# Output projection, plain blocks and first product pair of a hybrid decoder block: the passage between them in another order

## The chip, the core and the metric

The kernel runs on one core of a Trainium2 chip. Five engines work on their own queues: TensorE (PE) multiplies, VectorE (DVE) and ScalarE (ACT) do elementwise work, GpSimd (POOL) and SyncE (SP) issue transfers here. Each queue is worked off in order, and instructions wait for each other by semaphores. The metric is the time of one execution in microseconds (us); lower is better.

## What is computed

A decoder block over 1024 positions of width 1024, float32: a state-space branch and a gated convolution branch, merged by gates and projected, then a squared-ReLU MLP. Cut to what matters here (the mixer's inner part left out):

```python
def rmsnorm(x, g):
    var = jnp.mean(x * x, axis=-1, keepdims=True)
    return x * lax.rsqrt(var + NORM_EPS) * g
...
    merged = jax.nn.sigmoid(g_ssm) * y_a + jax.nn.sigmoid(g_conv) * y_b
    return jnp.einsum('bsd,de->bse', merged, w_out)
...
def squared_relu_mlp(xn, w_ff1, w_ff2):              # w_ff1: 1024 x 4096
    h = jax.nn.relu(jnp.einsum('bsd,df->bsf', xn, w_ff1))
    return jnp.einsum('bsf,fd->bsd', h * h, w_ff2)
...
    h = h + mixer_block(rmsnorm(h, norm_mix_g), ...)
    h = h + squared_relu_mlp(rmsnorm(h, norm_mlp_g), w_ff1, w_ff2)
    return rmsnorm(h, norm_final_g)
```

## The kernel before

Everything is kept transposed: 128 channels on the partitions, positions along the row, in two halves of 512 (`HS[0]`, `HS[1]`). A float32 product is made of three TensorE passes: each operand is split into a high part (ScalarE copies it to a rounded type) and a low part (VectorE subtracts the high part), and high x high, low x high and high x low are added up in one PSUM bank (a 128x512 float32 buffer; there are eight). So a split is always a ScalarE instruction followed by a VectorE one.

The order of each engine's queue is the order in which the code is written; nothing reorders it. The stretch that the change touches goes like this.

Gate jobs (`glu`, the last eight jobs of the main loop at L736): each loads a weight block three jobs ahead on SP (`w_load`, L77), splits the next job's block (`w_split`, L83) and multiplies 48 times. At the start of the last job the first of eight blocks of w_out is loaded and split (`wo_cut(0)`, L745), and eight loads of the residual `h` (`load_x`, L708) follow on SP.

Output projection (`wo_half`, L860): two passes, one for each half of the positions, of eight tiles of 24 matmuls (tile `pw`). In the first pass each step loads and splits the block of the next step (L864). After each tile VectorE adds the result to `h`, POOL writes it out (`hd`), ScalarE squares it, VectorE adds the square to `ssum`. During the second pass (`during_second`, L910) the first half is normalised: `rms_steps(0)` sums `ssum` over channels on TensorE (L604), takes the inverse root in some small VectorE steps and spreads it with two matmuls (L639) to `r2`; `normed` (L903) multiplies `h` (a scalar_tensor_tensor) and `put` (L891) splits the result into the operands `xh` and `xl` of blocks B11 and B21. Also there the four plain weight blocks are loaded and split (`plain_cut`, L927; tiles `rp`, `hp`, `lp`).

Plain blocks (`plain`, L938): four of the 32 column blocks of w_ff1 are computed directly, each in two halves (tile `pp`, 24 matmuls), then relu on ScalarE (L947, tile `r`), square on VectorE (L935, tile `f`), written out by POOL (`h2d`). The four first halves come first, with the second half's rms and normalisation between them (operands B12, B22). Then the eight-bank PSUM pool is closed and opened again as a pool of six and one of two (`seeds`, L970 to L974), and the four second halves follow. Between those stand the sums for the pairs: `t1`, `n2`, `t3`, `t4` (L1047 to L1064), differences of the four operand blocks, each split by `put`.

Pairs (L1101): the other 28 column blocks go two at a time, as 2x2 block products with seven half-size products (P1 to P7, Strassen-Winograd) instead of eight. Their weights are sums of the raw blocks `g` (`group_load`, L984), formed and split by `group_steps` (L993) in six steps: sums `gs1`, `gs2`, high parts `gh0` to `gh3`, low parts `gl0` to `gl3`. The later pairs' steps are taken during the pair before; those of the first are taken in two goes, the second behind all sums (L1065). The bank of P1, `pa`, is copied by ScalarE to a seed bank (L1109) before P2 is added onto it. The last stage multiplies by w_ff2.

## Time and profile before

| | |
|---|---|
| three timed runs | 1528.18, 1528.91 (median), 1530.28 us |
| the profiled run | 1529.01 us, its span 1527.2 us |
| mean granted TensorE clock | 0.986 of full speed |
| TensorE, matmuls | 1479.5 us busy, 97% of the span |
| VectorE | 920.3 us, 60% |
| ScalarE | 492.1 us, 32% |
| POOL | 111.6 us, 7% |

The span runs from the first to the last instruction of one profiled execution; the time of a run has some two microseconds around it. Busy time says how much an engine ran, not what it held up: TensorE fills 97% of the span, so the other engines matter only where TensorE waits for them. In the span cut into 40 slices, TensorE's row shows 9 (90% or more) nearly throughout, but 7 and 5 in two slices in the middle (840 to 916 us), where its granted clock falls as well. That is the passage described above.

### The profile page before, as it was taken

Reading aid. Unit: us, or ns where it says so; the run is one execution under the profiler, and the core shown is the slowest. Engines: PE = TensorE matmul, PEld = TensorE weight load, DVE = VectorE, ACT = ScalarE, POOL = GpSimd, SP = SyncE. Lnnn points to the kernel's source line nnn. Section 1 sums busy time; section 2 is a strip of 40 time slices with the busy share of each in tenths; the row PEclk is TensorE's granted clock in tenths of the full one; section 3 lists DMA queues with packets and bytes.
Section 4 is the critical chain, followed back from the end, with each engine's and each line's share of the span. In section 5 each row is a group of like instructions: output and inputs, shape, how many; then the busy total and the mean of one; then the engine's idle time right before and its main releaser. Section 6 shows DMA issues by size and latency. Waiting matters only on the chain.

```text
span 1527.2 us, 16887 instructions
## 1 busy us (share of the span) xinstructions
PE 1479.5 (97%) x6707; PEld 1226.6 (80%) x6707; DVE 920.3 (60%) x1459; ACT 492.1 (32%) x698; POOL 111.6 (7%) x270
## 2 busy tenths in 40 slices
PE   9989999999999999999999759999999999999997
PEld 7868888888888888888787648888887888888897
DVE  6578587687886776366446565555545444444555
ACT  5642332233223337232223333333333212121234
POOL 5840000000000000000000001111110000000000
PEclk9999999999999999999999879999999999999998
DMA  5011111111111111113412223333245323232302
GB/s 209 28 42 42 55 42 42 42 42 52 45 42 42 42 42 56 42 56 113 177 42 97 89 83 111 111 110 111 83 178 187 111 97 111 97 110 98 96 13 98
DMA packets 38623, 125.43 MB, mean 82 GB/s; under 512 B 4624, under 2 KB 9104, under 8 KB 38544
## 3 DMA queue, kind: packets, MB, share of 16 engines
q1 hardware_dynamic: 32144, 103.38, 20.0%
q0 software_dynamic: 6400, 20.98, 3.5%
q8 instruction: 52, 0.85, 0.2%
q14 instruction: 27, 0.22, 0.0%
HBM read 99.17 MB, written 25.17 MB: 81 GB/s over the span
## 4 chain that ended last, share of the span: by engine, by line
PE 85%; DVE 8%; ACT 4%; DMA 1%; issue 1%; SPq 0%; DVEq 0%; ACTq 0%
PE ps L128 8%; PE ps L130 8%; PE ps L129 8%; PE pf L129 7%; PE pf L130 7%; PE pf L128 7%; PE seed L1039 2%; PE seed L1040 2%; PE seed L1041 2%; PE pc L128 2%; PE pc L130 2%; PE pc L129 2%; PE pg L129 2%; PE pg L128 2%; PE pg L130 2%; PE pe L1041 2%
## 5 line engine op out<-in xcount | busy, mean ns | idle before, releaser
L128 PE MATMUL ps<-xh,wh 128*128 128x512 f32 x656 | 259.9, 396 | 1.2 <-ACT wh L88 1.2
L130 PE MATMUL ps<-xh,wl 128*128 128x512 f32 x656 | 256.1, 390 | 1.6 <-DVE wl L89 1.6
L129 PE MATMUL ps<-xl,wh 128*128 128x512 f32 x656 | 255.3, 389 | 0.0
L129 PE MATMUL pf<-fl,hw 128*128 128x512 f32 x448 | 174.3, 389 | 0.0
L128 PE MATMUL pf<-fh,hw 128*128 128x512 f32 x448 | 174.3, 389 | 0.0
L130 PE MATMUL pf<-fh,lw 128*128 128x512 f32 x448 | 174.3, 389 | 0.0
L1172 DVE TENSOR_TENSOR ha<-pf,ha 128x512 f32<-128x512 f32 x112 | 76.5, 689 | 145.7 <-PE pf L130 145.6
L130 PEld LDWEIGHTS ps<-xh,wl 128*128 128x128 f32 x656 | 123.1, 188 | 29.2 <-DVE wl L89 3.5
L128 PEld LDWEIGHTS ps<-xh,wh 128*128 128x128 f32 x656 | 123.3, 188 | 28.6 <-ACT wh L88 2.3
L129 PEld LDWEIGHTS ps<-xl,wh 128*128 128x128 f32 x656 | 123.3, 188 | 25.4
L722 ACT ACTIVATE hw<-rw 128x1024 fp32r<-128x1024 f32 x32 | 34.0, 1061 | 231.2 <-DMA rw<-in_w 210.8
L89 DVE TENSOR_TENSOR wl<-wr,wh 128x1024 fp32r<-128x1024 f32 x57 | 69.8, 1224 | 59.2 <-ACT wh L88 59.2
L128 PEld LDWEIGHTS pf<-fh,hw 128*128 128x128 f32 x448 | 84.1, 188 | 17.6
L129 PEld LDWEIGHTS pf<-fl,hw 128*128 128x128 f32 x448 | 84.1, 188 | 17.5
L130 PEld LDWEIGHTS pf<-fh,lw 128*128 128x128 f32 x448 | 84.1, 188 | 17.4
L935 DVE TENSOR_TENSOR f<-r 128x512 f32<-128x512 f32 x36 | 24.9, 691 | 102.6 <-ACT r L1123 51.9
L88 ACT ACTIVATE wh<-wr 128x1024 fp32r<-128x1024 f32 x57 | 59.6, 1047 | 52.3 <-PE pc L129 21.0
L868 POOL DMA_DIRECT2D hd<-h x16 | 8.9, 559 | 719.1 <-ACT ssum L870 638.6
L128 PE MATMUL pw<-mh,hwo 128*128 128x512 f32 x128 | 50.7, 396 | 3.1 <-ACT hwo L722 3.1
L130 PE MATMUL pw<-mh,lwo 128*128 128x512 f32 x128 | 50.5, 394 | 0.1
L129 PE MATMUL pw<-ml,hwo 128*128 128x512 f32 x128 | 50.3, 393 | 0.0
L128 PE MATMUL pc<-vh,wh 128*128 128x512 f32 x128 | 49.9, 390 | 0.0
(375 smaller groups left out, 2991.9 us busy)
## 6 DMA issues: line engine op xcount, KB each, us to landing
wr<-in_win SPq DMA_DIRECT2D x41, 512.0 KB, 3.6
hr<-h2d SPq DMA_DIRECT2D x32, 512.0 KB, 6.1
rw<-in_w SPq DMA_DIRECT2D x32, 512.0 KB, 3.5
g<-in_w SPq DMA_DIRECT2D x28, 512.0 KB, 3.7
h2d<-f POOLq DMA_DIRECT2D x36, 256.0 KB, 2.6
h2d<-c POOLq DMA_DIRECT2D x28, 256.0 KB, 2.8
wr<-in_wco SPq DMA_DIRECT2D x8, 512.0 KB, 3.4
wr<-in_wglu SPq DMA_DIRECT2D x8, 512.0 KB, 3.5
```

Source lines behind the costliest of these rows:

```text
L88: A.activation(hi, r, AF.Copy)
L89: V.tensor_sub(lo, r, hi.bitcast(F32))
L128: T.matmul(ps, wh[:, j, :], xh[:, cols], start=start and i == 0, stop=False)
L129: T.matmul(ps, wh[:, j, :], xl[:, cols], start=False, stop=False)
L130: T.matmul(ps, wl[:, j, :], xh[:, cols], start=False, stop=stop and i == n - 1)
L722: A.activation(hi, r, AF.Copy)
L868: nc.gpsimd.dma_start(hd[i][:, c], h[i][:, c])
L935: V.tensor_mul(f, r, r)
L1039: T.matmul(p, wh[:, kb, :], xh, start=first and kb == 0, stop=False, skip_group_check=True)
L1040: T.matmul(p, wh[:, kb, :], xl, start=False, stop=False, skip_group_check=True)
L1041: T.matmul(p, wl[:, kb, :], xh, start=False, stop=kb == 3, skip_group_check=True)
L1172: V.tensor_add(h[e][:, HS[hh]], p, h[e][:, HS[hh]])
```

## The change

Five things are changed, all between the gate jobs and the second pair:

- The loads of w_out's blocks are parted from their splits (`wo_load`, `wo_cut`). Six blocks are loaded during the gate jobs, five of them also split there, into tiles of the large pool; the last two loads follow the h loads.
- `put` issues the high part at once and queues the low part: the two newest stay queued (`low`, `lows`).
- Column sums of the second half's rms move into the middle of the first plain block, the spreading matmuls into the middle of the second; the plain products take the operands in the order in which they are normalised.
- The first pair's weights: the loads, and three of their six steps, now come before the second half's normalisation (`group_first`). The sums follow in single steps (`sum_steps`), `n2` first for all four, then `t3` and `t4`; the last steps of the weights come in the first pair. The second halves go in the order 2, 3, 0, 1 as before, with the seed matmuls ahead of the last.
- The PSUM pool of eight stays to the end; the seeds are two of its banks.

The diff, without its empty lines:

```diff
@@ -723,9 +723,18 @@
         V.tensor_sub(lo, r, hi.bitcast(F32))
         return hi, lo
+    wo_raw = {}
+    def wo_load(i):
+        if i < 8:
+            r = unit(f"rwo{i}").rearrange("p (k m) -> p k m", k=8)
+            nc.sync.dma_start(r, wo[i])
+            wo_raw[i] = r
     def wo_cut(i):
-        mk = lambda nm: unit(nm, F32R).rearrange("p (k m) -> p k m", k=8)
-        wo_w.append(cut(raw_load(wo[i], f"wo{i}"), f"wo{i}", mk))
+        if i < 8:
+            mk = lambda nm: unit(nm, F32R).rearrange("p (k m) -> p k m", k=8)
+            wo_w.append(cut(wo_raw.pop(i), f"wo{i}", mk))
     def in_proj(n):
         ps = [bank(f"ps{n}_{i}") for i in range(2)]
@@ -741,8 +750,11 @@
         w_split(n + 1)
         w_load(n + 3)
         w = parts.get(n)
+        if k == "glu" and i >= 2:
+            wo_load(i - 2)
+            if i > 2:
+                wo_cut(i - 3)
         if n == n_main - 1:
-            wo_cut(0)
             for e in range(4):
                 load_x(e)
         if k == "gs" and i == 1:
@@ -860,8 +872,9 @@
     def wo_half(hh, after):
         c = HS[hh]
         for i in range(8):
-            if hh == 0 and i < 7:
-                wo_cut(i + 1)
+            if hh == 0:
+                wo_load(i + 6)
+                wo_cut(i + 5)
             p = bank(f"pw{hh}_{i}")
             products(p, wo_w[i], range(8), merged, c)
             V.tensor_add(h[i][:, c], p, h[i][:, c])
@@ -894,7 +907,15 @@
         o = slice((kb % 2) * HALF, (kb % 2 + 1) * HALF)
         hi, lo = (t[:, o] for t in xop[name, kb // 2])
         A.activation(hi, src, AF.Copy)
-        V.tensor_sub(lo, src, hi.bitcast(F32))
+        low.append((lo, src, hi))
+        lows(2)
+    low = []
+    def lows(keep=0):
+        while len(low) > keep:
+            lo, src, hi = low.pop(0)
+            V.tensor_sub(lo, src, hi.bitcast(F32))
     def operand(name, kb):
         o = slice((kb % 2) * HALF, (kb % 2 + 1) * HALF)
@@ -905,20 +926,20 @@
         V.scalar_tensor_tensor(h[k][:, c], h[k][:, c], col(C_G2 + k), r2[:, c], op0=ALU.mult, op1=ALU.mult)
         put(f"B{1 + k // 4}{1 + hh}", k % 4, h[k][:, c])
-    steps = [None, None]
+    rms = {}
     def during_second(i):
         if i == 0:
-            steps[0] = rms_steps(0)
-            next(steps[0])
+            rms[0] = rms_steps(0)
+            next(rms[0])
         elif i == 1:
-            next(steps[0])
+            next(rms[0])
         elif i < 6:
             for k in ((0, 1), (4, 5), (2, 3), (6, 7))[i - 2]:
                 normed(k, 0)
-        if i >= 5:
             if i == 5:
-                plain_cut(0)
+                lows()
+        if i >= 4:
             plain_cut(i - 4)
@@ -935,43 +956,29 @@
         V.tensor_mul(f, r, r)
         nc.gpsimd.dma_start(h2d[b][:, HS[hh]], f)
-    def plain(b, hh):
+    def plain(b, hh, beside=None, mid=None):
         p = bank(f"pp{b}_{hh}")
         wh, wl = plain_w[b]
-        for k in range(8):
+        for i, k in enumerate((0, 1, 4, 5, 2, 3, 6, 7)):
             xh, xl = operand(f"B{1 + k // 4}{1 + hh}", k % 4)
-            T.matmul(p, wh[:, k, :], xh, start=k == 0, stop=False)
+            T.matmul(p, wh[:, k, :], xh, start=i == 0, stop=False)
             T.matmul(p, wh[:, k, :], xl, start=False, stop=False)
-            T.matmul(p, wl[:, k, :], xh, start=False, stop=k == 7)
+            T.matmul(p, wl[:, k, :], xh, start=False, stop=i == 7)
+            if i == 3 and mid:
+                mid()
+        if beside:
+            beside()
         r = half(f"r{b}_{hh}")
         A.activation(r, p, AF.Relu)
         square_out(b, hh, r)
     wo_half(0, lambda i: None)
     wo_half(1, during_second)
-    for b in range(N_PLAIN):
-        plain(b, 0)
-        if b == 0:
-            plain_cut(3)
-            steps[1] = rms_steps(1)
-            next(steps[1])
-        elif b == 1:
-            next(steps[1])
-            for k in (0, 1, 4, 5):
-                normed(k, 1)
-        elif b == 2:
-            for k in (2, 3, 6, 7):
-                normed(k, 1)
-    psum_ctx.close()
-    psum2 = ctx.enter_context(tc.tile_pool(name="psum2", bufs=6, space=bass.MemoryType.PSUM))
-    pseed = ctx.enter_context(tc.tile_pool(name="pseed", bufs=1, space=bass.MemoryType.PSUM))
-    psum = psum2
-    seeds = [pseed.tile([P, HALF], F32, tag=f"s{i}", name=f"seed{i}") for i in range(2)]
     def ltile(nm, dt):
         return late.tile([P, S], dt, tag="l", name=nm).rearrange("p (a k m) -> p a k m", a=2, k=4)
@@ -1040,33 +1047,66 @@
             T.matmul(p, wh[:, kb, :], xl, start=False, stop=False, skip_group_check=True)
             T.matmul(p, wl[:, kb, :], xh, start=False, stop=kb == 3, skip_group_check=True)
-    for b in (2, 3, 0, 1):
-        plain(b, 1)
-        if b == 2:
-            group_load(0)
-            for kb in range(4):
-                t = half(f"t1_{kb}")
-                V.tensor_sub(t, h[kb][:, HS[0]], h[kb][:, HS[1]])
-                put("t1", kb, t)
-        elif b == 3:
-            prep = group_steps(0)
+    def sum_steps():
+        for kb in range(4):
+            t = half(f"t1_{kb}")
+            V.tensor_sub(t, h[kb][:, HS[0]], h[kb][:, HS[1]])
+            put("t1", kb, t)
+            yield
+        for kb in range(4):
+            b11, b12 = (h[kb][:, HS[i]] for i in range(2))
+            V.tensor_sub(b12, b12, h[kb + 4][:, HS[1]])
+            V.tensor_sub(b11, b11, b12)
+            put("n2", kb, b11)
+            yield
+        for kb in range(4):
+            put("t3", kb, h[kb][:, HS[1]])
+            b21 = h[kb + 4][:, HS[0]]
+            V.tensor_sub(b21, b21, h[kb][:, HS[0]])
+            put("t4", kb, b21)
+            yield
+        lows()
+        yield
+    sums = sum_steps()
+    def some(n, *ks):
+        def f():
+            for k in ks:
+                normed(k, 1)
+            if ks and n:
+                lows()
+            for _ in range(n):
+                next(sums, None)
+        return f
+    def rms_first():
+        rms[1] = rms_steps(1)
+        next(rms[1])
+    def group_first():
+        for _ in range(3):
             next(prep)
-            next(prep)
-        if b in (3, 0, 1):
-            for kb in {3: (0,), 0: (1, 2), 1: (3,)}[b]:
-                b11, b12 = (h[kb][:, HS[i]] for i in range(2))
-                b21, b22 = (h[kb + 4][:, HS[i]] for i in range(2))
-                V.tensor_sub(b12, b12, b22)
-                V.tensor_sub(b11, b11, b12)
-                put("n2", kb, b11)
-                put("t3", kb, b12)
-                V.tensor_sub(b21, b21, b11)
-                put("t4", kb, b21)
-    for _ in prep:
-        pass
+    group_load(0)
+    prep = group_steps(0)
+    plain(0, 0, group_first, rms_first)
+    plain(1, 0, some(0, 0, 1, 4, 5), lambda: next(rms[1]))
+    plain(2, 0, some(0, 2, 3, 6, 7))
+    lows()
+    plain(3, 0, some(3))
+    plain(2, 1, some(3))
+    plain(3, 1, some(2))
     group_load(1)
+    plain(0, 1, some(2))
+    seeds = [bank(f"seed{i}") for i in range(2)]
     for s in seeds:
         T.matmul(s, mhalf, operand("B11", 0)[0], start=True, stop=True)
+    plain(1, 1, some(1))
+    for _ in sums:
+        pass
+    prep0 = prep
     def finish_c21(g):
         r = half(f"r21_{g}")
@@ -1102,6 +1142,9 @@
         last_g = g == N_GROUP - 1
         b0 = N_PLAIN + 2 * g
         group_load(g + 2)
+        if g == 0:
+            for _ in prep0:
+                pass
         prep = group_steps(g + 1)
         seed = seeds[g % 2]
         pa, pe = bank(f"pa{g}"), bank(f"pe{g}")
```

Three places show what this does to the queues. In the rows of the changed kernel the line numbers are its own.

SP's queue from the last gate loads to the projection (`wr`: gate weights; `rwo`: raw blocks of w_out). Before:

```order
L80 DMA wr56_5192<-in_wglu 128x1024
L717 DMA rwo0_5412<-in_wo 128x1024
L710 DMA h0_5418<-in_x_t 128x1024
L710 DMA h1_5420<-in_x_t 128x1024
L710 DMA h2_5422<-in_x_t 128x1024
L710 DMA h3_5424<-in_x_t 128x1024
L710 DMA h4_5496<-in_x_t 128x1024
L710 DMA h5_5498<-in_x_t 128x1024
L710 DMA h6_5500<-in_x_t 128x1024
L710 DMA h7_5502<-in_x_t 128x1024
L717 DMA rwo1_5506<-in_wo 128x1024
```

and now:

```order
L731 DMA rwo0_5042<-in_wo 128x1024
L80 DMA wr55_5118<-in_wglu 128x1024
L731 DMA rwo1_5120<-in_wo 128x1024
L80 DMA wr56_5200<-in_wglu 128x1024
L731 DMA rwo2_5202<-in_wo 128x1024
L731 DMA rwo3_5282<-in_wo 128x1024
L731 DMA rwo4_5362<-in_wo 128x1024
L731 DMA rwo5_5438<-in_wo 128x1024
L710 DMA h0_5444<-in_x_t 128x1024
L710 DMA h1_5446<-in_x_t 128x1024
L710 DMA h2_5448<-in_x_t 128x1024
```

The blocks 0 to 5 moved ahead of the h loads; 6 and 7 follow behind h7.

ScalarE's queue while the second half is normalised (`xhB...`: high parts; `r2_0`, `r3_0`: relu of the plain blocks' first halves). Before:

```order
L896 ACTIVATE xhB220_6191<-h5_5498 128x512
L947 ACTIVATE r2_0_6223<-pp2_0_6198 128x512
L896 ACTIVATE xhB121_6229<-h2_5422 128x512
L896 ACTIVATE xhB121_6229<-h3_5424 128x512
L896 ACTIVATE xhB221_6237<-h6_5500 128x512
L896 ACTIVATE xhB221_6237<-h7_5502 128x512
L947 ACTIVATE r3_0_6269<-pp3_0_6244 128x512
L947 ACTIVATE r2_1_6308<-pp2_1_6283 128x512
```

and now:

```order
L909 ACTIVATE xhB220_6202<-h5_5524 128x512
L973 ACTIVATE r1_0_6209<-pp1_0_6167 128x512
L909 ACTIVATE xhB121_6240<-h2_5448 128x512
L909 ACTIVATE xhB121_6240<-h3_5450 128x512
L909 ACTIVATE xhB221_6248<-h6_5526 128x512
L909 ACTIVATE xhB221_6248<-h7_5528 128x512
L973 ACTIVATE r2_0_6255<-pp2_0_6214 128x512
L909 ACTIVATE xht10_6289<-t1_0_6287 128x512
L909 ACTIVATE xht10_6289<-t1_1_6292 128x512
L909 ACTIVATE xht11_6297<-t1_2_6295 128x512
L973 ACTIVATE r3_0_6301<-pp3_0_6262 128x512
```

The relus moved back behind later pieces: `r3_0` now stands behind the high parts of three sums.

VectorE's queue at the first pair's weights (`gs`, `gl`). Before, they end the passage:

```order
L1059 TENSOR_TENSOR h3_5424<-h3_5424,h7_5502 128x512
L1060 TENSOR_TENSOR h3_5424<-h3_5424 128x512
L897 TENSOR_TENSOR xln21_6433<-h3_5424,xhn21_6432 128x512
L897 TENSOR_TENSOR xlt31_6437<-h3_5424,xht31_6436 128x512
L1063 TENSOR_TENSOR h7_5502<-h7_5502,h3_5424 128x512
L897 TENSOR_TENSOR xlt41_6442<-h7_5502,xht41_6441 128x512
L1019 TENSOR_TENSOR gs2_0_6484<-gs1_0_6367,g0_0_6313 128x512
L1020 TENSOR_TENSOR gs2_0_6484<-g0_0_6313,g0_1_6315 128x512
L1006 TENSOR_TENSOR gl10_6487<-gs1_0_6367,gh10_6372 128x1024
```

and now they come right behind the rms, ahead of the normalisation:

```order
L631 TENSOR_TENSOR n1d1_6134<-ident_73,n1v_6123 128x512
L1017 TENSOR_TENSOR gs1_0_6148<-g0_1_6103 128x512
L1018 TENSOR_TENSOR gs1_0_6148<-gs1_0_6148,g0_0_6101 128x512
L1013 TENSOR_TENSOR gl00_6155<-g0_0_6101,gh00_6151 128x1024
L1026 TENSOR_TENSOR gs2_0_6157<-gs1_0_6148,g0_0_6101 128x512
L1027 TENSOR_TENSOR gs2_0_6157<-g0_0_6101,g0_1_6103 128x512
L1013 TENSOR_TENSOR gl10_6160<-gs1_0_6148,gh10_6153 128x1024
L956 TENSOR_TENSOR f0_0_6164<-r0_0_6162 128x512
L926 SCALAR_TENSOR_TENSOR h0_5444<-h0_5444,pt_72,r2_5531 128x512
L926 SCALAR_TENSOR_TENSOR h1_5446<-h1_5446,pt_72,r2_5531 128x512
L926 SCALAR_TENSOR_TENSOR h4_5522<-h4_5522,pt_72,r2_5531 128x512
```

The weights moved from behind the last sum to ahead of the second half's normalisation. On ScalarE the copy of P1 to the seed keeps its place at the end of the passage, behind the last high parts (`xht3`, `xht4`) and two weight pieces:

```order
L973 ACTIVATE r1_1_6476<-pp1_1_6442 128x512
L909 ACTIVATE xht31_6467<-h3_5450 128x512
L909 ACTIVATE xht41_6472<-h7_5528 128x512
L1008 ACTIVATE gh20_6492<-gs2_0_6157 128x1024
L1008 ACTIVATE gh30_6496<-g0_1_6103 128x512
L1152 ACTIVATE seed0_6438<-pa0_6500 128x512
```

Here nothing moved but the piece of `n2` ahead, which now comes earlier.

## Rows read from the trace of the kernel before

**Rows 1.** TensorE's timeline around the first tile of the output projection: start, us, instruction.
```profile
717.79 0.39 PE L129 MATMUL pg<-zl,wh 128*128 128x512 f32 x1
...
726.86 0.39 PE L130 MATMUL pw<-mh,lwo 128*128 128x512 f32 x1
730.34 0.69 PE L128 MATMUL pw<-mh,hwo 128*128 128x512 f32 x1 [3.10 <-ACT hwo L722]
...
733.89 0.40 PE L129 MATMUL pw<-ml,hwo 128*128 128x512 f32 x1
```

**Rows 2.** TensorE's timeline between the first and the second plain block.
```profile
820.57 0.39 PE L945 MATMUL pp<-xhB,lp 128*128 128x512 f32 x1
822.91 1.02 PE L604 MATMUL pr<-ones,ssum 128*128 128x1 f32 x8 [1.95 <-DVE ssum L874]
```

**Rows 3.** TensorE's timeline from the last first-half block to the second half.
```profile
840.47 0.39 PE L945 MATMUL pp<-xhB,lp 128*128 128x512 f32 x1
847.78 0.79 PE L943 MATMUL pp<-xhB,hp 128*128 128x512 f32 x1 [6.93 <-ACT r L947]
...
853.44 0.40 PE L944 MATMUL pp<-xlB,hp 128*128 128x512 f32 x1
```

**Rows 4.** TensorE's timeline in the first pair.
```profile
875.70 0.39 PE L1040 MATMUL pe<-xlt,gh 128*128 128x512 f32 x1
893.43 0.80 PE L1041 MATMUL pe<-xht,gl 128*128 128x512 f32 x1 [17.34 <-DVE gl L1006]
...
897.82 0.39 PE L1039 MATMUL pa<-xhB,gh 128*128 128x512 f32 x1
```

**Rows 5.** Stretches: us, busy time by engine, granted clock, DMA share, GB/s.
```profile
731.00:736.00 5.00, 4.85 (x17) 3.54 (x16) 2.37 (x3) 1.58 (x2) 0.79 (x1) 0.71 1.00 402
...
818.00:823.00 5.00, 3.05 (x15) 2.23 (x14) 2.52 (x3) 2.65 (x4) 0.54 (x1) 1.00 0.59 185
...
848.00:853.50 5.50, 5.50 (x14) 4.30 (x15) 0.57 (x1) 0.00 (x0) 0.54 (x1) 0.51 0.12 48
```

**Rows 6.** ScalarE's timeline in the plain blocks.
```profile
818.39 1.06 ACT L722 ACTIVATE hp<-rp 128x1024 fp32r<-128x1024 f32 x1 [1.36 <-DMA rp<-in_w]
...
846.61 0.63 ACT L896 ACTIVATE xhB<-h 128x512 fp32r<-128x512 f32 x1 [1.42 <-DVE h L905]
847.15 0.58 ACT L947 ACTIVATE r<-pp 128x512 f32<-128x512 f32 x1
```

**Rows 7.** VectorE's timeline, second pass of the projection to the first pair.
```profile
788.36 0.69 DVE L867 TENSOR_TENSOR h<-pw,h 128x512 f32<-128x512 f32 x1 [3.75 <-PE pw L130]
...
790.41 0.75 DVE L905 SCALAR_TENSOR_TENSOR h<-h,pt,r 128x512 f32<-128x512 f32 x1
...
819.49 1.23 DVE L723 TENSOR_TENSOR lp<-rp,hp 128x1024 fp32r<-128x1024 f32 x1 [1.73 <-ACT hp L722]
820.63 0.68 DVE L867 TENSOR_TENSOR h<-pw,h 128x512 f32<-128x512 f32 x1
822.07 0.69 DVE L874 TENSOR_TENSOR ssum<-ssum,sq 128x512 f32<-128x512 f32 x1 [0.76 <-ACT sq L873]
...
826.33 1.29 DVE L631 TENSOR_TENSOR n1d<-ident,n1v 128x512 fp32r<-128x512 f32 x2
...
868.52 0.68 DVE L1059 TENSOR_TENSOR h<-h,h 128x512 f32<-128x512 f32 x1
869.24 0.69 DVE L1060 TENSOR_TENSOR h<-h 128x512 f32<-128x512 f32 x1
```

**Rows 8.** DMA issues from 640 to 900 us by median landing, and one transfer of the chain.
```profile
rwo<-in_wo SPq DMA_DIRECT2D x8, 512.0 KB, 9.0
g<-in_w SPq DMA_DIRECT2D x8, 512.0 KB, 3.7
...
814.66 3.65 DMA rp<-in_w
```

**Rows 9.** VectorE's timeline in a gate job.
```profile
700.15 0.69 DVE L846 TENSOR_TENSOR s<-pg,s 128x512 f32<-128x512 f32 x1 [1.90 <-PE pg L130]
```

## The prediction

> **What bounds the kernel now.** I read the span's table of engines first: TensorE is busy for 1479.5 of 1527.2 us, so a microsecond is won only where TensorE stands still or runs at half rate. The list of waits by engine then names four stops that lie one after the other in the stretch from 727 to 898 us, and TensorE's timeline there gives their size. At full rate a 512-column matmul starts every 0.227 us (40 steps from 717.79 to 726.86) [rows 1]; I count a stop from the start that was due to the start at which the full rate is back, less the matmuls done in between.
>
> First stop, weights of the output projection: due at 727.08, started at 730.34, full rate again at 733.89 with seven matmuls done: 6.81 - 1.59 = 5.2 us [rows 1]. Second, the sum of squares of the second half: due at 820.80, started at 822.91, 2.1 us [rows 2]. Third, the second half of the plain blocks: due at 840.70, started at 847.78, full rate at 853.44 after 13: 12.74 - 2.95 = 9.8 us [rows 3]. Fourth, the low part of the first pair's second weights: due at 875.93, started at 893.43, full rate at 897.82 after 10: 21.89 - 2.27 = 19.6 us [rows 4]. Together 36.7 us; the same matmuls are computed before and after, so this is all that there is to win here. From 897.82 on the queue of TensorE is unchanged, and what is won ahead of it moves the end by as much.
>
> Part of each stop is the clock: 0.71 granted after the first, 0.51 after the third, but 1.00 around the second, whose gap was 2.1 us [rows 5].
>
> **Step lengths.** VectorE: a 128x512 instruction starts 0.61 us after the one before it when it does not need it (its 0.69 less 0.08: 819.49 + 1.23 is followed at 820.63), 0.72 when it does (868.52 to 869.24), 0.67 after the normalising one of 0.75, 1.15 after a 128x1024 one. An add of h with its square on ScalarE puts the sum 1.44 behind the add (820.63 to 822.07), and TensorE's column sums started 0.84 behind that [rows 2, 7]. ScalarE: 0.54 from one 512-column instruction to the next, 0.95 after a 1024-column one; a split's low part starts 1.10 after its high part (818.39 to 819.49); TensorE or VectorE go on 0.63 after the start of the ScalarE instruction that they wait for (847.15 to 847.78) [rows 3, 6, 7]. All times below are those of the trace of before, so that the first stop is still in them; it is taken off at the end.
>
> **First stop: gone, +5.2.** It came from one queue: SP issued w_out's first block, then eight loads of h, of which four wait for the last gate job's matmuls, and only then the second block. Six blocks now stand ahead of the h loads, and five are split before the projection starts. The price is a split more in each gate job: 1.15 us of VectorE where it idles 1.90 in one place alone [rows 9] of a job of 48 matmuls, 10.9 us, and 0.95 of ScalarE. Blocks six and seven are issued where the second was and are needed six tiles (33 us) later. Cost nothing, as long as that idle time covers it.
>
> **Second stop: 2.1 becomes 0.8.** The column sums now stand 12 matmuls inside the first plain block. The adds of the second pass follow TensorE every 5.44 us from 788.36 [rows 7], so the last is due at 815.56. Holding low parts back by two takes the ScalarE round trips out of the normalisation, and a step of the pass then costs 1.44 + 0.61 + 2 x 0.67 + 2 x 0.61 = 4.6 us, less than 5.44; but the weight splits come into steps 4 to 7. Step 4 adds at 799.24; its second normalisation starts at 802.57, the high part of that on ScalarE 0.78 later, the split's high part after it at 803.89, so the split's low part at 804.98 and the next add at 806.12 instead of 804.68. Step 5 carries two low parts more and a split (1.44 + 0.61 + 2 x 0.67 + 4 x 0.61 + 1.15 = 7.0), so the next add is at 813.1; step 6 only add, sum and split (0.78 + 0.54 + 1.10 + 1.15 = 3.6), so the last add is at 816.6 and its sum at 818.07. TensorE is ready at 815.36 + 12 x 0.227 = 818.08 and goes on at 818.91: a wait of 0.8.
>
> **Third stop: 9.8 becomes nothing, with 2 us to spare.** The last of the four first-half blocks no longer has to be emptied before the second half may begin: the pool of eight banks stays, and the next block needs a bank emptied long before. What is left are the operands. In front of them VectorE now forms the first pair's weights. The last plain split ends at 820.26 and lets the pair's second raw block be issued, which lands 3.7 us later [rows 8], at 823.96; the inverse rms, 4.7 us from the first column sum to the end of its last VectorE step (822.91 to 827.62) [rows 2, 7], is done at 823.6. Six weight instructions take 0.72 + 3 x 0.61 + 2 x 1.15 = 4.9 us, to 828.8. From the first square to the low part of the last operand are 18 starts, ten at 0.61 and eight at 0.67, plus twice 0.67 because a square's relu stands in ScalarE's queue behind the high part of the normalisation just before: 12.8, so 841.6, done at 842.3. TensorE starts the second half at 815.36 + 4 x 5.44 + 0.8 + 1.5 (the two rms steps) = 839.4 and needs that last operand at 844.4.
>
> **Fourth stop: 19.6 becomes 3.3.** Those weights are ready, but ScalarE reaches its copy of the first product late. In its queue the copy stands behind two weight pieces and the high part of the last sum. From 841.6 VectorE has 34 starts to that sum's subtraction: 34 x 0.61 + 4 x 0.11 (dependent) + 5 x 0.67 (squares behind a relu) = 24.5, so 866.1, done 866.85. Then ScalarE: 0.54 + 0.95 + 0.54, copy at 868.9, TensorE free at 869.5. It wants the bank back at 839.4 + 4 x 5.44 + 0.45 + 5.44 = 867.0. Wait 2.5 us. What the clock adds lies between nothing (gap of 2.1) and 1.6 (first stop: 3.55 us for seven matmuls, less 1.59, less about 0.35 for a low part that came late); I take half, 0.8. The other products of this pair find their operands, and the later pairs stand in the queues as before.
>
> **Sum.** 36.7 - 0.8 - 2.5 - 0.8 = 32.6 us. The profiled run took 1529.01 us with 1527.2 of span, 0.1 above the median of the runs; 1529.0 - 32.6 = 1496.4. The walk has some 90 starts; 0.02 us on each is 1.8 us on the wait of 2.5, hence 1494.5 to 1498.5 for this case.
>
> **Rivals.** *No wait left.* If VectorE's walk is 3 us shorter than I make it, both waits vanish: 1529.0 - 36.7 = 1492.3. For it: two of my round trips may overlap. Against: each is taken from a row.
>
> *The pair's weights hold the queue.* The new wait on the raw block stands at the head of VectorE's queue, and the normalisation behind it. If the block takes the 9.0 us that eight blocks in flight took in this stretch [rows 8], all behind it comes 5.3 later: the last operands 3.4 late, the copy's wait 4.5 and its clock 2.7 (third stop): 36.7 - 0.8 - 3.4 - 4.5 - 2.7 = 25.3, so 1503.7. For it: POOL writes h at the same time. [...] Against: a plain block issued at 814.66 was in use at 818.39 beside such a write [rows 6, 8].
>
> *The first stop stays.* If the early blocks are held up by slots, the change doesn't do that part: 1496.4 + 5.2 = 1501.6. Against: the loads that now come first wait for readers a whole job back.
>
> *Slower.* The split added to five gate jobs could push the next job's own split past its start, with TensorE stopped in each. It decides from 32.6 / 5 = 6.5 us a job on; at 7.5 the time is 1496.4 + 37.5 = 1533.9. Against: VectorE's idle 1.90 ahead of one product [rows 9], more than the 1.15 added.
>
> [...]
>
> **How the numbers follow.** Forecast 0.53; no wait 0.15; weights hold the queue 0.21; first stop stays 0.06; slower 0.02; something unseen 0.03. Leaving out the slow side and the tail of the third case, 8 in 10 lie from 1492 to 1504.5. A measurement of this kernel tells about 0.2%, 3 us, from no change: faster by more 0.95, within 0.02, slower 0.03.
>
> **What would show it.** Right: no TensorE wait on hwo; the wait on ssum under 1.5 us; none on r of the plain blocks; the one on gl of the pair gone and in its place one on ScalarE's copy of pa, 1 to 4 us. Wrong: a VectorE wait on g of several us ahead of the normalisation; a wait on xlB; a stop in a gate job; or a granted clock under 1 from 727 to 860.

## The result, and the profile after

| | before | changed |
|---|---|---|
| median of four runs, us | 1529.6 (1528.2 to 1531.4) | 1494.45 (1493.2 to 1495.3) |
| profiled run, us (span) | 1529.01 (1527.2) | 1494.97 (1493.2) |
| mean granted TensorE clock | 0.986 | 0.994 |
| TensorE, busy | 1479.5 us, 97% | 1473.2 us, 99% |
| first matmul of the output projection to first of P6 | 178.93 us | 146.53 us |

The changed kernel takes 0.977 of the time before (95% interval 0.9752 to 0.9786), 35 us less; 1496.4 was forecast. The last line of the table is the measure for all that follows. I call it the stretch: from the first `pw` matmul to the first matmul of P6 in the first pair, the first group behind the last stop of either kernel. It got 32.4 us shorter, where the forecast had 32.6. Behind it both traces take the same 618.85 us to the last group of matmuls; in front of it both kernels run the same matmuls, and the changed one arrived 1.62 us earlier (720.02 for 721.64). More on that at experiment 12.

In the list of waits by engine, TensorE from 640 to 900 us (line, what it waited for, total us, times, longest), two lines are left of the four; the columns are as before:

```profile
PE pa L1046 <- ACT seed L1152: 2.0, 1, 2.0
PE pr L604 <- DVE ssum L887: 0.5, 1, 0.5
```

TensorE's timeline of the changed kernel (start, us, instruction) has the places that answer to [rows 1, 2, 4]. The first two steps, across the place of the former first stop (from the last matmul of the projection's first tile to the second tile), are 0.23 and 0.22 us. The column sums were due at 810.96 + 0.23 = 811.19 and started 0.64 later. P2 was due at 859.95, started 2.16 later, and P6 began at 866.55, where 12 matmuls at full rate, 0.227 us each, end 2.72 behind P2's start; so another 1.72 is the clock.

```profile
725.23 0.39 PE L130 MATMUL pw<-mh,lwo 128*128 128x512 f32 x1
725.46 0.39 PE L128 MATMUL pw<-mh,hwo 128*128 128x512 f32 x1
725.68 0.39 PE L129 MATMUL pw<-ml,hwo 128*128 128x512 f32 x1
...
810.96 0.39 PE L967 MATMUL pp<-xhB,lp 128*128 128x512 f32 x1
811.83 1.02 PE L604 MATMUL pr<-ones,ssum 128*128 128x1 f32 x8 [0.48 <-DVE ssum L887]
...
859.72 0.39 PE L1048 MATMUL pe<-xht,gl 128*128 128x512 f32 x1
862.11 0.50 PE L1046 MATMUL pa<-xhB,gh 128*128 128x512 f32 x1 [2.00 <-ACT seed L1152]
...
866.55 0.39 PE L1046 MATMUL seed<-xhn,gh 128*128 128x512 f32 x1
```

The stretches (us; busy time and count of PE, PEld, DVE, ACT, POOL; granted clock, DMA share, GB/s) show that clock: 1.00 through the former first stop, 0.52 behind P2's gap. They answer to [rows 5].

```profile
725.40:731.40 6.00, 6.00 (x28) 4.95 (x28) 2.22 (x3) 1.58 (x2) 0.79 (x1) 1.00 0.84 340
...
859.70:862.10 2.40, 0.41 (x2) 0.00 (x0) 2.40 (x4) 2.40 (x5) 0.00 (x0) 1.00 0.32 121
862.90:866.20 3.30, 3.30 (x9) 2.53 (x8) 2.51 (x4) 1.67 (x3) 0.00 (x0) 0.52 0.50 159
```

Why P2 waits is read on ScalarE. Its timeline shows the copy of P1's bank (`seed<-pa`, L1152) behind the high part of the last sum, which waited for VectorE, and two weight pieces, without idle time between them, and P2 goes on 0.63 behind the copy's start:

```profile
859.47 0.63 ACT L909 ACTIVATE xht<-h 128x512 fp32r<-128x512 f32 x1 [1.45 <-DVE h L1066]
860.01 1.04 ACT L1008 ACTIVATE gh<-gs 128x1024 fp32r<-128x1024 f32 x1
860.96 0.61 ACT L1008 ACTIVATE gh<-g 128x512 fp32r<-128x512 f32 x1
861.48 0.58 ACT L1152 ACTIVATE seed<-pa 128x512 f32<-128x512 f32 x1
```

VectorE's timeline at the places that the forecast walked through: the last add and its sum, the first weight sum (which waited 0.99 for its raw block), the last operand's low part (the second of two), the subtraction of the last sum.

```profile
809.55 0.68 DVE L880 TENSOR_TENSOR h<-pw,h 128x512 f32<-128x512 f32 x1
810.99 0.69 DVE L887 TENSOR_TENSOR ssum<-ssum,sq 128x512 f32<-128x512 f32 x1 [0.76 <-ACT sq L886]
...
816.93 0.69 DVE L1017 TENSOR_TENSOR gs<-g 128x512 f32<-128x512 f32 x1 [0.99 <-DMA g<-in_w]
...
833.81 1.29 DVE L918 TENSOR_TENSOR xlB<-h,xhB 128x512 fp32r<-128x512 f32 x2
...
858.75 0.69 DVE L1066 TENSOR_TENSOR h<-h,h 128x512 f32<-128x512 f32 x1
```

### The profile page after: what moved, and what is told of

Same layout as the page of the kernel before. It is cut to its first block, busy times and chain, and to the rows that moved or that the text cites. A ratio compares the mean times of both kernels' runs of the same rounds, so it can differ in the third digit from the quotient of the medians.

```text
span 1493.2 us, 16892 instructions
## 1 busy us (share of the span) xinstructions
PE 1473.2 (99%) x6707; PEld 1224.3 (82%) x6707; DVE 917.6 (61%) x1459; ACT 491.3 (33%) x698; POOL 111.0 (7%) x270
## 4 chain that ended last, share of the span: by engine, by line
PE 87%; DVE 7%; ACT 4%; issue 1%; DMA 1%; SPq 0%; DVEq 0%; ACTq 0%
PE ps L128 8%; PE ps L130 8%; PE ps L129 8%; PE pf L129 7%; PE pf L130 7%; PE pf L128 7%; PE seed L1046 3%; PE seed L1048 2%; PE seed L1047 2%; PE pc L128 2%; PE pg L129 2%; PE pg L128 2%; PE pc L130 2%; PE pc L129 2%; PE pg L130 2%; PE pa L1046 2%
## 5 line engine op out<-in xcount | busy, mean ns | idle before, releaser
L128 PEld LDWEIGHTS pf<-fh,hw 128*128 128x128 f32 x448 | 84.1, 188 | 17.5
L129 PEld LDWEIGHTS pf<-fl,hw 128*128 128x128 f32 x448 | 84.1, 188 | 17.5
L130 PEld LDWEIGHTS pf<-fh,lw 128*128 128x128 f32 x448 | 84.1, 188 | 17.3
L130 PE MATMUL pc<-vh,wl 128*128 128x512 f32 x128 | 49.8, 389 | 0.0
```

The costliest lines, as they stand in the source:

```text
L128: T.matmul(ps, wh[:, j, :], xh[:, cols], start=start and i == 0, stop=False)
L129: T.matmul(ps, wh[:, j, :], xl[:, cols], start=False, stop=False)
L130: T.matmul(ps, wl[:, j, :], xh[:, cols], start=False, stop=stop and i == n - 1)
```

## The experiments

The forecast went stop by stop. The experiments go edit by edit: six parts of the change are taken out of the changed kernel, each alone, and two ways of removing the last stop are tried. Not taken out by themselves are the order of the operands in the plain products, the order of the sums and the plain weight split that now comes a step earlier. Two traces of one kernel give the stretch within 0.25 us (experiments 4 and 12); the runs behind a median spread over 2 to 4 us. The medians of the kernel before beside them were 1529.1, 1528.1 and 1527.9 us.

| experiment | median, us | stretch, us | TensorE's waits in the stretch, us |
|---|---|---|---|
| changed kernel | 1494.45 | 146.53 | ssum 0.5, copy 2.0 |
| 1 e1_copy_ahead | 1492.0 | 142.67 | ssum 0.5 |
| 2 e8_copy_ahead_rms_later | 1491.6 | 142.02 | none |
| 3 e9_one_piece | 1493.0 | 144.11 | ssum 0.5, copy 1.2 |
| 4 e7_after_again | 1495.1 | 146.39 | ssum 0.5, copy 1.8 |
| 5 e11_lows_at_once | 1512.1 | 161.87 | ssum 3.5, copy 10.6 |
| 6 e2_loads_as_before | 1498.7 | 151.31 | hwo 3.3, ssum 0.5, copy 1.8 |
| 7 e3_weights_late | 1500.5 | 151.06 | ssum 0.5, gl 5.8 |
| 8 e4_two_pools | 1499.0 | 150.78 | ssum 0.5, r of pp 5.4 |
| 9 e10_sums_behind_blocks | 1498.2 | 149.45 | ssum 0.5, copy 4.4 |
| 10 e5_rms_between | 1496.6 | 147.26 | copy 3.4 |
| 11 e6_second_block_twice | 1498.5 | 149.97 | ssum 0.5, xlB 0.9, copy 3.9 |
| 12 e0_before_again | 1529.5 (one run) | 178.68 | hwo 3.2, ssum 1.7, r of pp 6.9, gl 17.3 |

**1. The copy ahead of the pieces.** ScalarE's copy of P1 is issued before the last sum step and the weight pieces.

```diff
     plain(1, 1, some(1))
-    for _ in sums:
-        pass
...
-        if g == 0:
-            for _ in prep0:
-                pass
...
         A.activation(seed, pa, AF.Copy, scale=-1.0)
+        if g == 0:
+            for _ in sums:
+                pass
+            for _ in prep0:
+                pass
```

> The changed kernel (1494.45 us) with one thing moved: ScalarE's copy of the first product is issued ahead of the last operand sums and of the weight pieces gh20 and gh30, and not behind them. In the changed kernel TensorE was due for P2 at 859.95 us, started at 862.11 and had its full rate back at 866.55 with 12 matmuls done: 2.16 us of wait and 1.72 of slow clock. Theory A: the wait is ScalarE's queue alone and the low clock follows from the gap, so both go: 1494.45 - 3.9 = 1490.6, no TensorE wait on the copy, granted clock 1.00 from 845 to 875 us. Theory B: the clock falls there for another reason (or did not fall in most runs), so only the wait goes: 1494.45 - 2.2 = 1492.3. Theory C: the pieces that are now later are missed by P3 or P7, and a wait on gl or xlt takes the place of the one removed: 1494 or more.

The stretch is 3.86 us shorter, theory A to 0.1; no wait on the copy is left, no other came in its place, and the clock stays at 1.00 from 845 to 875 us. ScalarE's timeline shows the copy released by TensorE itself:

```profile
858.10 0.58 ACT L1147 ACTIVATE seed<-pa 128x512 f32<-128x512 f32 x1 [0.20 <-PE pa L1048]
...
860.41 1.04 ACT L1008 ACTIVATE gh<-gs 128x1024 fp32r<-128x1024 f32 x1
```

The medians differ by 2.5 us only. Which of the two numbers a typical run saves, 3.9 or the bare wait, is taken up at experiment 4.

**2. Besides, the column sums three matmuls later.**

```diff
-            if i == 3 and mid:
+            if i == 4 and mid:
```

> The kernel with the copy of the first product ahead, and besides the column sums of the second half three matmuls later in the first plain block (behind 15, not 12). The wait of 0.64 us on ssum goes (due 811.18, sums ready for 811.83, three matmuls are 0.68): 1490.6 - 0.65 = 1489.9. Against it: the inverse root comes no later, since VectorE and not TensorE sets its start; if it does come later, the normalisation of the second half slips by under 0.1 us.

Another 0.65 us off the stretch, as expected. TensorE now does not wait at all between the projection and P6, and 178.93 - 142.02 = 36.9 us is what the four stops of the kernel before cost (36.7 were counted). The median of this kernel, 1491.6 us, is 0.976 of the kernel before (0.9741 to 0.9773) and 2.9 us under the changed kernel's; between it and experiment 1 the medians decide nothing.

**3. The copy behind one piece.** A shorter gap at P2, to size what the clock takes.

```diff
         if g == 0:
-            for _ in prep0:
-                pass
+            next(prep0)
...
         A.activation(seed, pa, AF.Copy, scale=-1.0)
+        if g == 0:
+            for _ in prep0:
+                pass
```

> The changed kernel with ScalarE's copy of the first product behind one weight piece, gh20, and ahead of gh30: the gap at P2 should be 0.52 us shorter, 1.64 for 2.16. Theory A: the clock falls behind it all the same: the stretch from the projection's first matmul to P6 is 146.5 - 0.5 = 146.0 us, 1494 in all. Theory B: behind a gap of 1.6 it does not: 144.3 us, 1492.3.

TensorE's timeline has P2 due at 862.11 and started at 863.43, a gap of 1.32 (0.3 shorter than meant):

```profile
861.88 0.39 PE L1048 MATMUL pe<-xht,gl 128*128 128x512 f32 x1
863.43 0.50 PE L1046 MATMUL pa<-xhB,gh 128*128 128x512 f32 x1 [1.16 <-ACT seed L1151]
```

The stretch from 862.9 to 866.2 us, the columns as above, has the clock at 1.00, where the changed kernel had 0.52. Theory B.

```profile
862.90:866.20 3.30, 2.77 (x12) 2.31 (x13) 3.27 (x6) 2.47 (x5) 0.00 (x0) 1.00 0.13 29
```

**4. The changed kernel once more.** No edit.

> The changed kernel itself, profiled a second time. In its first profile the clock fell behind the 2.16 us gap at P2 (1.72 us), and fell too behind a gap near 77 us that the traces of other kernels here show with the same length and no fall. Theory A: the fall belongs to the gap, so the stretch from the first matmul of the output projection to the first of P6 is 146.5 us again. Theory B: at gaps of this size it is a matter of the single execution; most runs of this kernel showed a mean clock of 0.996, as the kernel without that gap does: a stretch of 144.8 us is then as likely, and the copy ahead of the pieces is worth 2.2 us in most runs and 3.9 in some. Median 1494.5 either way.

The gap at P2 is 1.98 us and the clock falls behind it again (0.51 from 862.9 to 866.2); the stretch is 146.39. Experiment 6 has a gap of 1.99 at the same place, and it falls there too (1.3 us). That speaks for theory A at this place. Against it stand the mean clocks of whole runs: 0.994 in both profiled runs and 0.996 in the other six, where the kernel of experiment 1 shows 0.996 or 0.995; but both profiled runs had one more fall near 77 us (last section). So whether every run pays the 1.7 us is not settled, and the copy ahead saves between 2.2 and 3.9.

**5. Low parts at once.** The part of the change that looked smallest.

```diff
-        lows(2)
+        lows()
```

> The changed kernel with no low part held back: each follows its high part at once, as before. Theory A: holding them back by two is the largest part of the change. Without it each of the 28 operand pieces of VectorE waits for ScalarE some 0.66 us: the last sum of squares comes 2 to 3 us later (wait on ssum near 3), the last operand of the second half 5.9 later against 2.1 to spare (a wait on xlB of 3 to 4, with 1 to 2.7 of clock), the sums some 13 later (the wait on the copy grows by 5 to 7): 1494.45 + 13.5 = 1508, between 1503 and 1513. Theory B: VectorE idles there anyway, and the round trips fill idle time: 1494.5 to 1497.

The stretch is 15.3 us longer, by far the most that one edit gives back. VectorE's timeline shows why: of the 32 low parts, 28 find it idle for 0.70 to 0.76 us until ScalarE is done, here in the normalisation of the second half (first four rows, this experiment). Held back by two, none of the 32 has idle time in front of it (last two rows, the changed kernel).

```profile
827.46 0.75 DVE L926 SCALAR_TENSOR_TENSOR h<-h,pt,r 128x512 f32<-128x512 f32 x1
828.91 0.69 DVE L918 TENSOR_TENSOR xlB<-h,xhB 128x512 fp32r<-128x512 f32 x1 [0.70 <-ACT xhB L909]
829.52 0.75 DVE L926 SCALAR_TENSOR_TENSOR h<-h,pt,r 128x512 f32<-128x512 f32 x1
830.96 0.69 DVE L918 TENSOR_TENSOR xlB<-h,xhB 128x512 fp32r<-128x512 f32 x1 [0.70 <-ACT xhB L909]
```

```profile
828.74 0.75 DVE L926 SCALAR_TENSOR_TENSOR h<-h,pt,r 128x512 f32<-128x512 f32 x1
829.40 0.69 DVE L918 TENSOR_TENSOR xlB<-h,xhB 128x512 fp32r<-128x512 f32 x1
```

Theory A, but over the stretch its sum was 1.8 us short (13.5 for 15.3; the median, 1512.1, is 4.1 above the 1508 expected), and the places were wrong: the column sums started 3.7 us late with 2.8 of clock behind them, TensorE was then late enough for the operands, so the wait on xlB did not come, and P2's gap grew by 8.6, not 5 to 7.

**6. Loads as before.** The first block behind the last gate job's start, each further one a tile ahead.

```diff
-            r = unit(f"rwo{i}").rearrange("p (k m) -> p k m", k=8)
-            nc.sync.dma_start(r, wo[i])
-            wo_raw[i] = r
+            wo_raw[i] = raw_load(wo[i], f"wo{i}")
...
-        if k == "glu" and i >= 2:
-            wo_load(i - 2)
-            if i > 2:
-                wo_cut(i - 3)
         if n == n_main - 1:
+            wo_load(0)
+            wo_cut(0)
...
-                wo_load(i + 6)
-                wo_cut(i + 5)
+                wo_load(i + 1)
+                wo_cut(i + 1)
```

> The changed kernel with the blocks of the output projection loaded and split as before: the first at the start of the last gate job, ahead of the loads of h, each further one a tile ahead. Theory: the first stop comes back with its 5.2 us and nothing else moves, since all that follows it follows TensorE: 1494.45 + 5.2 = 1499.7, a TensorE wait of 3.1 on hwo, and 88.45 + 5.2 = 93.7 us from the first matmul of the projection to the first of the plain blocks. Rival: the splits that now stand in the gate jobs cost something there, and the stretch of the gate jobs gets shorter without them: less than 5.2 in all.

The same stop at the same tile, 5.3 us from the first matmul to the plain blocks (93.78 for 88.44), 4.8 over the stretch, since the gap at P2 with its clock is 0.6 shorter here (1.99 and 1.3 us). The splits in the gate jobs cost nothing: between 640 and 720 us TensorE is busy all the time in the changed kernel as in the one before (80.00 of 80.00 us, granted clock 1.00 in both).

```profile
727.40 0.39 PE L130 MATMUL pw<-mh,lwo 128*128 128x512 f32 x1
731.06 0.79 PE L128 MATMUL pw<-mh,hwo 128*128 128x512 f32 x1 [3.27 <-ACT hwo L722]
```

**7. The first pair's weights late.** One step behind the third block, two behind all sums, as before.

```diff
-    plain(0, 0, group_first, rms_first)
+    plain(0, 0, None, rms_first)
...
     plain(3, 1, some(2))
+    next(prep)
...
     for _ in sums:
         pass
+    for _ in range(2):
+        next(prep)
```

> The changed kernel with the first pair's weights formed where the kernel before formed them: the first step behind the third block of the second half, the next two behind all operand sums. Theory A: their early place is what removed the fourth stop, so its 15.7 us come back: about 1510, with a TensorE wait on gl of 13 to 17 us. Theory B: the fourth stop was VectorE's backlog of normalisation and sums, which the change shortened from the other end; forming the weights late only puts some 5 us of VectorE between the sums and P1. The inverse root arrives at 820.5 us, so the normalisation starts only 1.9 us earlier without the weights, the sums end near 860.6, gl0 near 861.8 where P1 wants it at 855: a wait of 6.9 and 2.7 of clock, against 3.9 in the changed kernel: 1494.45 + 5.7 = 1500.2, and no wait on the copy.

Theory B: TensorE's timeline has a gap of 6.0 us for gl in P1 (due 857.43); against experiment 1, which has no stop here, the stretch is 8.4 longer, so the clock takes 2.4. The wait on the copy goes: 4.5 us more than the changed kernel over the stretch (by the medians 6.1; 5.7 were expected). The 16 us that the fourth stop lost were not bought by this edit alone.

```profile
857.20 0.39 PE L1047 MATMUL pa<-xlB,gh 128*128 128x512 f32 x1
863.41 0.79 PE L1048 MATMUL pa<-xhB,gl 128*128 128x512 f32 x1 [5.83 <-DVE gl L1013]
```

**8. Two PSUM pools.** Closed and opened behind the four first halves.

```diff
     plain(3, 0, some(3))
+    psum_ctx.close()
+    psum2 = ctx.enter_context(tc.tile_pool(name="psum2", bufs=6, ...))
+    pseed = ctx.enter_context(tc.tile_pool(name="pseed", bufs=1, ...))
+    psum = psum2
+    seeds = [pseed.tile(...) for i in range(2)]
...
-    seeds = [bank(f"seed{i}") for i in range(2)]
```

> The changed kernel with the PSUM pool closed behind the four first halves and opened again as six banks and two, as before. Theory A: emptying the last first-half block is what made the third stop. Its relu stands at 837.47 us in ScalarE's queue, done 838.1, and the second half was started near 832.2: a wait of 5.9 and 2.7 of clock; ScalarE and VectorE follow 6.7 later, so the wait on the copy shrinks from 3.9 to about 0.3: 1494.45 + 8.6 - 3.6 = 1499.5. Theory B: the operands of the second half were the limit and the pool costs nothing: 1494.5, with the wait on the copy as it is.

Theory A. TensorE's timeline (first row) stops for the relu (L973), which in ScalarE's (the other two) stands behind three operand pieces. From the first `pp` to the first `pa` matmul it takes 54.0 us for 46.05, so the stop costs 8; the stop at P2 goes, since TensorE arrives later, and 4.25 us are left over the stretch.

```profile
838.02 0.79 PE L965 MATMUL pp<-xhB,hp 128*128 128x512 f32 x1 [5.39 <-ACT r L973]
```

```profile
835.65 1.83 ACT L909 ACTIVATE xht<-t 128x512 fp32r<-128x512 f32 x3 [2.56 <-DVE t L1054]
837.39 0.58 ACT L973 ACTIVATE r<-pp 128x512 f32<-128x512 f32 x1
```

**9. Sums behind the blocks.** The operand sums start behind the first block of the second half.

```diff
-    plain(3, 0, some(3))
-    plain(2, 1, some(3))
-    plain(3, 1, some(2))
+    plain(3, 0)
+    plain(2, 1)
+    some(4)()
+    plain(3, 1)
+    some(2)()
     group_load(1)
-    plain(0, 1, some(2))
+    plain(0, 1)
+    some(4)()
...
-    plain(1, 1, some(1))
+    plain(1, 1)
```

> The changed kernel with the operand sums behind the blocks of the second half (four steps behind the first, two, four and two behind the others), each behind that block's relu and square, as before; they started during the last first-half block. Theory A: VectorE then idles for the relus, from 835 to 838.5 us and behind each later square a little, and the last sum comes 2.5 to 4 later: the wait on the copy grows by as much, 1497.5. Theory B: nothing, since the waits on the relu are there either way: 1494.5.

Theory A: VectorE idles 3.15 us for one relu (row below), P2's gap is 4.6 us, the stretch 2.9 longer.

```profile
840.59 0.69 DVE L956 TENSOR_TENSOR f<-r 128x512 f32<-128x512 f32 x1 [3.15 <-ACT r L973]
841.20 1.89 DVE L1054 TENSOR_TENSOR t<-h 128x512 f32<-128x512 f32 x3
```

**10. The rms steps between the blocks.**

```diff
+    def between():
+        rms_first()
+        group_first()
+
+    def second():
+        next(rms[1])
+        some(0, 0, 1, 4, 5)()
+
-    plain(0, 0, group_first, rms_first)
-    plain(1, 0, some(0, 0, 1, 4, 5), lambda: next(rms[1]))
+    plain(0, 0, between)
+    plain(1, 0, second)
```

> The changed kernel with the two rms steps of the second half between the plain blocks, as before, and not inside them. Theory A: the place inside the block is what won the second stop; outside, the column sums stand at 813.9 us, the inverse root reaches VectorE 1.2 to 1.8 later than now; the third stop's 2 us to spare cover that, the wait on the copy grows by 2.1: 1494.45 - 0.65 + 2.1 = 1495.9. Theory B: the sums are ready earlier because the last adds of the projection come earlier, and the place is worth nothing or costs the 0.65 us wait on ssum: 1493.8, no wait on ssum, the wait on the copy as it is.

Between the two: the wait on ssum goes (so the earlier adds, not the place, won the second stop), and P2's gap grows by 1.4 (3.54 us). 0.7 us more over the stretch.

**11. The second raw block twice.** The price of a late block.

```diff
                 nc.sync.dma_start(r, w1[N_PLAIN + 2 * g + j])
+                if g == 0 and j == 1:
+                    nc.sync.dma_start(r, w1[N_PLAIN + 2 * g + j])
```

> The changed kernel with the first pair's second raw block loaded twice, the second transfer behind the first, so that VectorE's first weight sum waits some 3.7 us longer. This measures the price of the rival that the pair's weights hold VectorE's queue. Theory A: VectorE has no room there, so all behind it comes 3.7 later: the last operand of the second half is written at 838.9 where TensorE wants it at 837.3 (a wait of 1.6 on xlB, with up to 1.7 of clock), and the wait on the copy keeps what is left, 3.5 to 4.3: 3.7 to 4.5 in all, 1498.5. Theory B: waits on the relu leave VectorE room between, so less than 2 us arrive at P2 and none at the operands: under 1496.5.

VectorE waits 4.46 us for the block instead of 0.99. TensorE loses 1.5 to xlB in the second half's first block and 1.9 more at P2; the stretch is 3.44 longer. A delay of 3.5 on VectorE came out as 3.4 on TensorE: theory A. VectorE's timeline, then TensorE's:

```profile
820.69 0.70 DVE L1019 TENSOR_TENSOR gs<-g 128x512 f32<-128x512 f32 x1 [4.46 <-DMA g<-in_w]
```

```profile
838.30 0.50 PE L966 MATMUL pp<-xlB,hp 128*128 128x512 f32 x1 [0.91 <-DVE xlB L918]
```

**12. The kernel before once more.** No edit.

> The kernel before, profiled a second time. The changed kernel gained 32.4 us between the first matmul of the output projection and P6 of the first pair, and 1.6 more in front of it, where both kernels run the same code; its medians differ by 35.2. Theory A: the 1.6 is the start-up of a single execution, which in the traces so far put that first matmul anywhere from 720.0 to 722.5 us: here too it lies in that band, and the stretch is 178.9 again. Theory B: the changed kernel starts faster: 721.6 again, where both profiles of the changed kernel have 720.0 and 720.2. The gap at the column sums (2.1 us, no fall of the clock in the first profile) shows whether the clock falls there in another execution.

Theory A: in TensorE's timeline its first `pw` matmul stands at 722.24 and P6 begins at 900.92, a stretch of 178.68. Over all fourteen traces the first matmul lies between 720.02 and 722.48 us, in kernels whose matmuls up to there are the same; the two first profiles, 721.64 and 720.02, were 1.6 apart by that. That much is there from the first 12 us on: one and the same matmul of the first product (`ps`, the 21st of the program) starts at 9.43 us in the changed kernel and at 11.19 in the kernel before. The column sums waited 1.85 us here, again with no fall of the clock (steps of 0.23 us behind it).

```profile
722.24 0.39 PE L128 MATMUL pw<-mh,hwo 128*128 128x512 f32 x1
...
900.92 0.39 PE L1039 MATMUL seed<-xhn,gh 128*128 128x512 f32 x1
```

## Why the prediction was right, and where it was not

**What bounds the kernel: right.** Four stops worth 36.7 us were said to be all that there is. Experiment 2 has none of them and is 36.9 us shorter in the stretch.

**Step lengths and the walk: right.** Add 6.90 us to a time of the changed trace (its plain blocks start at 808.46 for 815.36) and compare with the forecast's:

| | forecast | measured |
|---|---|---|
| last add of the second pass | 816.6 | 816.45 |
| its sum of squares | 818.07 | 817.89 |
| first weight sum (raw block landed) | 823.96 | 823.83 |
| low part of the last operand | 841.6 | 841.31 |
| subtraction of the last sum | 866.1 | 865.65 |
| ScalarE's copy of P1 | 868.9 | 868.38 |
| P2 | 869.5 | 869.01 |

Some 90 starts add up to an error of 0.5 us.

**First stop: right.** 5.2 forecast, 5.28 measured (93.72 to 88.44), and experiment 6 brings it back alone.

**Second stop: right in size, wrong in its cause.** 0.8 forecast, 0.64 measured. But the forecast named the sums' place inside the block first; experiment 10 shows that the earlier adds do it. Its own walk had that: with TensorE free to go on with the sums from 818.91, sums left between the blocks, due at 820.80 before, would not have waited.

**Third stop: right.** No wait; the last operand, written by 835.1 us and needed about 837.3 (22 steps of 0.227 behind the second half's start near 832.3), had the 2 us to spare. Experiment 8 shows the pool close, experiment 11 the operands as what comes next.

**Fourth stop: mechanism right, its clock mis-sized.** The wait on ScalarE's copy was forecast at 2.5 us in P2, measured 2.16. The term that failed is the clock behind it: I took half of a range from nothing to 1.6, 0.8 us, and it is 1.72 in the first profile, above the whole range. No trace shows the half at P2: behind its gap the clock was 0.52 in the first profile and 0.51 in the second, and 1.00 behind the 1.32 of experiment 3. The half rested on the one gap of 2.1 us without a fall; the same trace has another, of 2.25 us near 107 us, and there the clock fell (last section). At the column sums it did not fall in either trace of the kernel before (2.1 and 1.85 us).

**The sum: right.** 36.7 - 0.64 - 2.16 - 1.72 = 32.2, with 32.4 measured. In the stretch the forecast was 0.2 us too good, and that it was so near is partly luck: 0.9 too little for the clock stood against waits 0.5 shorter than forecast and stops worth 0.2 more. That the time came out 1.95 below 1496.4 is the start, 1.62 between the two profiled runs, and 0.5 by which the profiled run stands above the median. The forecast had not considered that spread, up to 2.5 us, and 1494.45 lies 0.05 below the 1494.5 to 1498.5 that it gave its own case, about as far from 1496.4 as from the 1492.3 of the rival without a wait. The time could not tell the two apart; the wait on the copy in the trace does.

**The rivals.** *The pair's weights hold the queue*: the block landed 3.7 us behind its issue (813.19 to 816.91), as the lone one had, and the trace has 0.99 us of wait. A write of h ran beside it for the first 0.7 us only (it landed at 813.86), so a block beside a whole write was not tested by it; the pair's first block, with such a write inside its time, took 3.5. The price at 5.3 us late, 7.3 with the clock, was not tested; experiment 11 has 3.4 for 3.5. *No wait left*: VectorE's walk was not 3 us shorter than forecast but 0.5 (the table above); experiments 1 and 2 reach that case by another order on ScalarE. *First stop stays* and *slower*: no hwo wait, no stop in a gate job.

**What the forecast left out** is which edit buys what. It booked the fourth stop's gain under "those weights are ready". Taken out one at a time, the edits are worth: low parts held back 15.3, loads 4.8, the first pair's weights 4.5, one PSUM pool 4.25, sums earlier 2.9, rms inside the block 0.7. These add up to some 32.5, next to 32.4; that is not a law, since experiment 8 shows one stop hiding part of another. By the medians they are 17.7, 4.2, 6.1, 4.6, 3.8 and 2.2: the first is the largest either way, the order of the three behind it is not settled. Holding back was in the forecast's step lengths (0.61 for an independent step where a round trip to ScalarE stands in the kernel before), so the sum had it without the text saying that it was nearly half of the gain.

## What to carry to other kernels

Where two in-order engines hand work back and forth, issue the dependent half two items later: over 32 small pieces, 28 of which had waited, that was nearly half of the gain here (15.3 of 32.4 us). Count stops by the engine that bounds, but before you credit a gain to an edit, ask what else shortens the queue in front of the same wait. Compare traces over the stretch that an edit touches, from one landmark to another: what lies ahead of the edit, most of all the start of the program, moved these times by up to 2.5 us.

## What was not expected of the hardware

**A gap near 2 us had two prices.** At P2 the clock fell behind gaps of 1.98 (experiment 4, 0.51 granted), 1.99 (experiment 6, 1.3 us more in the stretch) and 2.16 us (the changed kernel, 0.52) and not behind 1.32 (experiment 3, 1.00); at the column sums of the kernel before it did not fall behind 2.1 (1.00 from 823 to 828 us) and 1.85 (experiment 12, steps of 0.23 us behind it). Near 107 us, in code that all kernels share, a gap of 2.23 to 2.26 us was followed by a fall in six traces: in the first profiles of both kernels 0.50 was granted (in the changed one from 109 to 111 us), and in experiments 3, 9, 11 and 12 pairs of matmuls came 0.85 us apart, which in the changed kernel came 0.44 apart ahead of its fall (108.00 to 108.44). In the kernel before (TensorE's timeline, then the stretch behind the gap):

```profile
106.55 0.39 PE L130 MATMUL ps<-xh,wl 128*128 128x512 f32 x1
109.03 1.03 PE L532 MATMUL psxr<-U,WT 128*128 128x256 f32 x2 [2.09 <-ACT WT L522]
```

```profile
109.30:112.60 3.30, 3.30 (x9) 2.56 (x9) 0.20 (x1) 3.02 (x6) 0.00 (x0) 0.50 0.00 0
```

Near 77 us, again in shared code, a wait of 1.15 to 1.18 us on a weight's high part and one of 0.53 to 0.60 on its low part were followed by a fall in the changed kernel twice and in experiment 10 (0.89 granted from 75 to 90 us in each), and by none in the kernel before twice and in experiments 3, 5, 6, 9 and 11 (1.00 in each). The stretch from 78.4 to 81 us, first in the changed kernel, then in experiment 1:

```profile
78.40:81.00 2.60, 2.60 (x7) 2.04 (x7) 2.54 (x5) 2.53 (x4) 2.60 (x10) 0.50 0.62 202
```

```profile
78.40:81.00 2.60, 2.60 (x12) 2.17 (x13) 2.53 (x6) 2.55 (x5) 2.52 (x11) 1.00 0.61 175
```

What decides it stays open. **Once it fell, the price did not go by the length of the gap in these traces:** 1.3 us behind 1.99 (experiment 6), 1.7 behind 2.16, 2.0 behind 3.26 (the first stop before, with a late low part in it), 1.7 behind 3.54 (experiment 10 against 2), 2.8 behind 3.7 (experiment 5), 2.4 behind 6.0 (experiment 7), 2.7 behind 7.1, 2.1 behind 17.5.
